# Turning position tiles in halves of 64 rows into a ring of five PSUM banks, and a reordered start, in a hybrid attention and Fourier encoder

## The chip, the cores and the metric

The kernel runs on one NeuronCore of one Trainium2 chip. The metric is the device time of one launch in microseconds (us). Engines are named as in the profile: PE (TensorE, matrix multiplication and transposes into PSUM), DVE (VectorE), ACT (ScalarE), POOL (GpSimd) and SP, which here only issues transfers. PSUM is the accumulator memory that PE writes; it has banks of 128 partitions by 512 float32 values.

## The reference

Two layers, each of which normalises its input, mixes it, multiplies it by a SiLU gate, maps it back and adds it to the residual. The rows are one prompt of 2048 positions and one sample of 512, both 1024 wide.

- Layer 0 is windowed attention, 16 query heads in 4 groups, with a position bias from a table (`rel_bias`) and a sink logit for each head.
- Layer 1 is Fourier mixing: for each of four groups of 256 channels, the real part of the two-dimensional discrete Fourier transform over positions and channels.
- A final normalisation follows: `x * rsqrt(mean(x*x) + 1e-6) * g`.

```python
def rmsnorm(x, g):
    xf = x.astype(jnp.float32)
    inv = lax.rsqrt(jnp.mean(xf * xf, axis=-1, keepdims=True) + RMS_EPS)
    return (xf * inv * g.astype(jnp.float32)).astype(x.dtype)
```

## The kernel before, in words

Lines are those of the kernel before, as in its profile. Almost every product of two float32 matrices is made of three products of a reduced float32 format: each operand is split into a high part (a copy on ACT) and a low part (a subtraction on DVE), and `matmul3` (L92, matmuls at L95) multiplies high by high, high by low and low by high. So an operand of PE is ready when ACT and then DVE are through with it.

**The order.** A scheduler writes each engine's instructions into one list when the kernel is built, and every engine runs its list in order. `after(a, b)` asks that `a` stands behind `b`, and `seq(name, ins)` chains instructions by a name; both give an order and not a wait between engines. What an instruction waits for follows from the tiles it reads and writes.

**The start** (L214 to L268). Twelve matmuls on an `idle` tile come first. The first key weight is requested in two halves, the first on SP ahead of everything else, the second on ACT; `g0s`, the norm's weight in a layout of 128 partitions by 8, is requested on ACT as single values; then the tiles `xk` of the transposed input come on SP. ACT and DVE make `h` (L220, L221) and the weight's parts (L253, L254), and PE multiplies them. `bias_rows` (L262) multiplies a one-hot matrix by the bias table in float32 (`bp`, L271). The rest of attention is not touched by the change, except that `bank` is shared.

**Position steps** (from about 1060 us the second layer, from about 1340 us these). The transform over positions is split into `k1` (0 to 8) and a second factor of 128. `position` (L1330) computes for one `k1` two tiles `u`, the rows `k1` and `16 - k1`; for 0 and 8 it is one tile each. It works in two halves of channels `hf`. In each half PE writes a cosine part `Ap` and a sine part `Bp` (six products each with two inputs, three with one), ACT copies from `Ap` (L1354, L1357), and DVE adds or subtracts `Bp` (L1358 to L1361). At the end DVE multiplies each `u` by its gate (L1364). The inputs `gp` are split by ACT and DVE at L1324, and their sums and differences (L1184, L1651 to L1655) are DVE's work too.

A `u` must be turned before PE can multiply it by the output weights. There are two forms:

- `step` (L1551) for p0 and p8, p4, and p2: it runs `position`, then `finish` for the first tile that is still pending from the step before, then `split_T` (L960, transposes L967) for the new tiles, then `finish` for the other pending tile. `finish` (L1384) is 48 matmuls `fo` of 512 columns, two additions to the residual on DVE (L1392), and `normed` (L1373): squares on ACT, a power on POOL, the scaling on DVE (L1376).
- `Outs` (L1397) for `k1` of 6, 1, 7, 3 and 5: `turn` (L1403, transposes L1409) turns the two tiles into four banks; `own` (L1416, L1417) makes the parts of one, `sums` (L1426, L1433) of their sums and differences; `products` (L1442) has the output products `Wo`, `Zo` and `Xo` with residual additions at L1457. Its hooks let the next `position` and the next tile's turns in between.

Each turned bank, `Ap` and `Bp` come from `bank` (L77), which takes the next of five tiles of one bank in the pool `psum3`. A full tile takes eight transposes of 128 by 128, so a block of two tiles takes 16.

Of the kernel before, what the change touches and what calls it, by code (L numbers as in the profile page):

```python
# [19 lines left out]
P = 128  # L20
# [8 lines left out]
WARM = 12  # L29
BIG = 1.0e30  # L30
# [12 lines left out]
def encoder(  # L43
# [19 lines left out]
    ACT.dma_start(g0s, g0.rearrange("(k p) -> p k", p=P))  # L63
# [13 lines left out]
    def bank(name):  # L77
        return banks[-1].tile([P, 512], F32, tag="bank", name=name)

# [12 lines left out]
    def matmul3(out, a, b, start, stop, more=False):  # L92

        for i, j in ((0, 0), (0, 1), (1, 0)):
            pe(PE.matmul(out, a[i], b[j], start=start and i + j == 0, stop=stop and i == 1, skip_group_check=more))  # L95
# [10 lines left out]
    def load_w(c, n, name, lo_engine=None, late=None, w32=None):  # L106
# [15 lines left out]
        if lo_engine is None:  # L122

            for i in range(4):
                cs = slice(i * 256, i * 256 + 256)
                POOL.tensor_tensor(w[:, 1, cs], w32[:, cs], f32(w[:, 0, cs]), ALU.subtract)
        else:
            lo_engine.tensor_tensor(w[:, 1], w32, f32(w[:, 0]), ALU.subtract)
# [4 lines left out]
    stage, res_tile, ready, chain, last_fetch = [], [], {}, {}, [None]  # L133
# [15 lines left out]
    def attention_phase():  # L149

        with ExitStack() as es:
# [6 lines left out]
            def stats(c):  # L158
# [7 lines left out]
                def one(i):  # L166

                    if i:
                        sq = ACT.activation(xs[i - 1], xs[i - 1], AF.Square, accum_out=ss[:, i - 1 : i])

                        if c > 1:
                            seq(ACT, sq)
                        else:
                            after(sq, last_exp[0])
                    while len(xs) < min(nt, i + (2 if c > 1 else 1)):
                        t = len(xs)
                        xs.append(xtile([P, D], F32, f"xs{c}_{t}"))
                        after(SP.dma_start(xs[t], x[tok + t * P : tok + (t + 1) * P, :]), last_exp[0])
# [5 lines left out]
            def spread(c, inv, place=None):  # L184
# [9 lines left out]
                for i0 in range(0, nt, step):  # L194
# [4 lines left out]
                    ACT.copy(invb[:, i0 * P : (i0 + m) * P], ps[:, : m * P])  # L199
                return invb  # L200

            def make_h(c, invb, between={}):
# [4 lines left out]
                for k in range(KD):  # L207
# [6 lines left out]
                    SP.dma_start(xk[:, :n], xT[k * P : (k + 1) * P, tok : tok + n])  # L214
# [8 lines left out]
                    after(lo, last_u[1])  # L223
                    hs.append((h[:, 0], h[:, 1]))
# [19 lines left out]
            last_u = [None, None]  # L244
# [4 lines left out]
            def half(i):  # L249
                cs = slice(i * 512, i * 512 + 512)  # L250
                (SP, ACT)[i].dma_start(wk32[:, cs], w_in[8, :, cs])
                return lambda: (
                    tc.keep_in_program_order(ACT.copy(wk[:, 0, cs], wk32[:, cs])),  # L253
                    DVE.tensor_tensor(wk[:, 1, cs], wk32[:, cs], f32(wk[:, 0, cs]), ALU.subtract),  # L254
                )

            halves = [half(i) for i in range(2)]
            halves[0]()
            early = [(wk[:, 0], wk[:, 1])]
            hs, halo = make_h(0, None, {0: halves[1], 3: lambda: early.append(load_w(0, 9, "k0_1", DVE))})  # L260

            def bias_rows():  # L262
# [4 lines left out]
                SP.dma_start(rb[:32], rel_bias)  # L267
                oh = ap.tile([33, 512], F32, tag="s", bufs=2, name="oh")  # L268
                SP.dma_start(oh, onehot)
                bp = bank("bp")  # L270
                PE.matmul(bp[:NH], rb, oh, start=True, stop=True)  # L271
# [5 lines left out]
                SP.dma_start(sk, bass.AP(sink.tensor, sink.offset, [[0, P], [1, NH]]))  # L277
# [24 lines left out]
            def kv_proj(c, hs, halo, norms=None, early=None):  # L302
# [40 lines left out]
                if norms is not None:  # L343
                    wv.append(load_w(c, 10, f"v{c}_0", DVE))
                    inv = norms()
# [7 lines left out]
                for i0 in range(0, len(blocks), 4):  # L353
# [10 lines left out]
                    for i, (src, c0, b) in enumerate(group):  # L364
# [3 lines left out]
                        if inv is not None:  # L368
                            sc = ap.tile([P, 1], F32, tag="vsc", bufs=2, name=f"vsc{c}_{b}")
                            DVE.tensor_scalar(sc, inv[:, i : i + 1], 0.5, None, ALU.mult)  # L370
# [63 lines left out]
            def attention(c, p, res, uTs):  # L434
# [17 lines left out]
                def sinks():  # L452
# [4 lines left out]
                    if p:  # L457
                        seq(ACT, ends)

# [330 lines left out]
            def first_norms():  # L790
                bias.extend(bias_rows())
                return [s() for s in stats(0)][-1]
# [140 lines left out]
    def fourier_phase(tail):  # L933
        with ExitStack() as es:
# [43 lines left out]

            def sumsq(src, name, place=lambda ins: None):
# [111 lines left out]
            def prod(out, a, b, ks, first):  # L1091

                for k in ks:
                    cs = slice(k * P, (k + 1) * P)
                    matmul3(out, (a[0][:, cs], a[1][:, cs]), b[k], first and k == 0, k == 3, not first)
# [129 lines left out]
            banks.append(es.enter_context(tc.tile_pool(name="psum3", bufs=5, space=PSUM, reuse_waits="tile")))  # L1225
# [76 lines left out]
            def gated(name, r, place):  # L1302
# [3 lines left out]
                if r[2] is None:  # L1306
                    SP.dma_start(s2, rows(src, (r[0] - off, r[1])))
# [20 lines left out]
            last_b = [None]  # L1328

            def position(name, tab, gr, gs, tiles, loads=None, parts=None, between=None, later=None):  # L1330
# [31 lines left out]
                for u, s2 in zip(us, s2s):  # L1362
                    if later is None:
                        DVE.tensor_tensor(u, u, s2, ALU.mult)  # L1364
# [8 lines left out]
            def normed(x2, r):  # L1373

                inv = sumsq(x2, f"f{r[0]}")
                after(DVE.scalar_tensor_tensor(x2, x2, inv[:, 0:1], gfb, ALU.mult, ALU.mult), last_b[0])  # L1376
                SP.dma_start(out_rows(r), x2)
# [6 lines left out]
            def finish(uT, r):  # L1384
                r0 = r[0]
                x2 = residual(r)
                for half in range(2):
                    ps = psum2.tile([P, 512], F32, tag="acc", name=f"fo{r0}_{half}")
                    for k in range(KD):
                        matmul3(ps, uT[k], wo[half * KD + k], k == 0, k == KD - 1)  # L1390
                    xs = x2[:, half * 512 : half * 512 + 512]
                    DVE.tensor_tensor(xs, xs, ps, ALU.add)  # L1392
                normed(x2, r)

            class Outs:  # L1397
# [6 lines left out]
                def turn(self, i, hf):  # L1404
                    u, r = self.us[i]
                    ps = bank(f"tr{self.n}_{i}{hf}")
                    for k in range(4):
                        c0 = (hf * 4 + k) * P
                        PE.transpose(ps[:, k * P : (k + 1) * P], u[:, c0 : c0 + P], ident)  # L1409
                    v = ps.rearrange("p (k q) -> p k q", k=4)  # L1410
                    self.ps[i, hf] = v[:, :, ::-1] if r[2] is not None else v

                def own(self, i, hf):
                    t = htile([P, 2, 512], F32R, f"tT{self.n}_{i}{hf}")
                    hi, lo = (t[:, j].rearrange("p (k q) -> p k q", k=4) for j in range(2))
# [4 lines left out]
                def sums(self, i):  # L1420
# [3 lines left out]
                    out = F[i] = self.pair[:, i in (2, 3)].rearrange("p (k q) -> p k q", k=4)  # L1424
# [8 lines left out]
                    DVE.tensor_tensor(out, a, b, op)  # L1433
# [3 lines left out]
                def operands(self):  # L1437
                    self.turn(0, 0)
                    self.own(0, 0)
                    self.turn(1, 0)  # L1440
                    self.turn(1, 1)
                    self.sums(1)  # L1442
                    self.sums(2)
                    self.turn(0, 1)
# [5 lines left out]
                def products(self, hooks, last=False):  # L1450
# [5 lines left out]
                    def add(t, half, ps):  # L1456
                        DVE.tensor_tensor(t[:, q[half]], t[:, q[half]], ps, ALU.add)  # L1457
# [16 lines left out]
                    add(xa, 0, X)  # L1474
                    hooks[2]()
                    if not last:
                        normed(xa, self.us[0][1])
                    else:

                        ya, yb = zt("ya"), zt("yb")  # L1480
                        turned = DVE.tensor_tensor(ya, xa, gfb, ALU.mult)
                        inv = sumsq(xa, "fa", lambda ins: after(ins, turned))
# [163 lines left out]
            G[0], G[8], G[4] = (r0, None), (r8, None), (g4r, g4s)  # L1646
            emit(0, 8)
# [47 lines left out]
            finish(*pend.pop(0))  # L1695
# [4 lines left out]
            def reads(k1):  # L1700

                gl = [zt(f"go{k1}_{i}") for i in range(2)]
                for hf in range(2):
                    cs = slice(hf * 512, hf * 512 + 512)
                    for g, src in zip(gl, god[k1]):
                        SP.dma_start(g[:, cs], src[:, cs])
# [129 lines left out]
```

## Time and profile before

| | us |
|---|---|
| median of 3 runs | 1582.07 (1581.98 to 1582.3) |
| profiled execution, its own time | 1581.38 |
| its span | 1579.4 |
| TensorE busy | 1569.0 |
| VectorE busy | 1153.0 |
| ScalarE busy | 876.5 |
| GpSimd busy | 446.1 |

The span is the time from the first to the last instruction in the trace of one execution. Busy is the time in which an engine has at least one instruction under way; matmuls overlap one another, so a matmul's duration (about 0.39 us for 512 columns) is longer than the time from its start to the next one's. In a row of the timeline, the first number is the start in us, the second the length of a run of like instructions, then come the engine, the line, the operation, the tile written and the tiles read, the shapes and the count; in square brackets is the time for which the engine stood idle before it, and what released it. The granted clock of TensorE was 0.999.

### The profile page before, as it was taken

The numbers are of one execution on the slowest core, as the hardware profiler recorded it, in microseconds if no ns is written. First come the engines' busy times: TensorE is split into PE (matmuls) and PEld (weight loads), VectorE is DVE, ScalarE is ACT, GpSimd is POOL, SyncE is SP. The second block draws the span as 40 slices with busy tenths as digits, with TensorE's granted clock in tenths as the row PEclk, the third lists the DMA queues.
The fourth block names the chain that finished last, engine by engine and source line by source line (L and its number), as shares of the span: only waits on it lengthen the run. The fifth ranks groups of instructions, "written<-read, shape, count | busy, mean of one in ns | idle before, by whom it ended". The sixth has DMA issues, their size and how long they took to land.

```text
span 1579.4 us, 27477 instructions
## 1 busy us (share of the span) xinstructions
PE 1569.0 (99%) x9755; PEld 1321.7 (84%) x9755; DVE 1153.0 (73%) x2790; ACT 876.5 (55%) x2093; POOL 446.1 (28%) x613
## 2 busy tenths in 40 slices
PE   9999999999999999999999999999999999999998
PEld 7888888888888888988888888888888888888886
DVE  6888655877548786378764587769878878989796
ACT  6688535776246784267852476646655554343242
POOL 2475642421404314024232242223112111010110
PEclk9999999999999999999999999999999999999999
DMA  7597696565856567656649556665557569557752
GB/s 292 199 335 287 228 361 211 207 248 204 297 209 221 207 236 264 232 203 225 248 165 334 216 209 223 248 252 203 204 207 255 178 220 405 187 182 299 282 206 80
DMA packets 101732, 373.89 MB, mean 237 GB/s; under 512 B 12267, under 2 KB 23019, under 8 KB 84188
## 3 DMA queue, kind: packets, MB, share of 16 engines
q1 hardware_dynamic: 82860, 298.04, 53.0%
q0 software_dynamic: 16400, 70.04, 11.5%
q10 hardware_dynamic: 2336, 4.07, 0.7%
q8 instruction: 77, 1.26, 0.3%
q14 instruction: 59, 0.48, 0.1%
HBM read 280.84 MB, written 91.26 MB: 236 GB/s over the span
## 4 chain that ended last, share of the span: by engine, by line
PE 96%; DVE 2%; ACT 1%; issue 0%; DMA 0%; POOL 0%; POOLq 0%; SPq 0%; DVEq 0%; ACTq 0%
PE gp L95 14%; PE qp L95 14%; PE spt L95 11%; PE op L95 7%; PE W L95 6%; PE av L557 6%; PE spt L472 6%; PE fo L95 5%; PE vp L95 3%; PE Wo L95 3%; PE Z L95 3%; PE pt L531 3%; PE z L95 2%; PE Zo L95 2%; PE X L95 2%; PE z L1079 1%
## 5 line engine op out<-in xcount | busy, mean ns | idle before, releaser
L95 PE MATMUL gp<-h,wg 128*128 128x512 f32 x960 | 237.6, 395 | 0.0
L95 PE MATMUL qp<-h,wq 128*128 128x512 f32 x960 | 237.0, 396 | 0.0
L491 DVE CUSTOM_DVE_ANT_0 S<-spt,b 128x385 f32<-128x385 f32 (+1 forms) x320 | 156.5, 528 | 104.3 <-PE spt L472 67.9
L95 PEld LDWEIGHTS gp<-h,wg 128*128 128x128 f32 x960 | 174.9, 188 | 37.2 <-issue 1.0
L95 PEld LDWEIGHTS qp<-h,wq 128*128 128x128 f32 x960 | 174.9, 188 | 36.5 <-issue 0.2
L499 ACT ACTIVATE S<-S 128x385 f32<-128x385 f32 (+1 forms) x320 | 188.8, 596 | 19.8 <-DVE S L491 19.5
L539 ACT CAST pts<-pt 128x384 fp32r<-128x384 f32 (+1 forms) x240 | 100.5, 458 | 168.2 <-PE pt L531 159.1
L540 DVE TENSOR_TENSOR pts<-pt,pts 128x384 fp32r<-128x384 f32 (+1 forms) x240 | 114.3, 520 | 23.4 <-ACT pts L539 22.2
L95 PE MATMUL spt<-wo,uT 128*128 128x512 f32 x480 | 120.5, 391 | 0.0
L581 POOL TENSOR_TENSOR uT<-o,uT 128x256 fp32r<-128x256 f32 x75 | 55.6, 741 | 229.0 <-ACT uT L580 228.9
L95 PE MATMUL op<-wo,uT 128*128 128x512 f32 x480 | 118.9, 391 | 0.0
L472 PE MATMUL spt<-kwin,qab 64*128 64x384 f32 (+1 forms) x960 | 118.4, 352 | 0.0
L557 PEld LDWEIGHTS av<-pts,v 128*128 128x128 f32 x576 | 101.4, 188 | 18.8
L557 PE MATMUL av<-pts,v 128*128 128x512 f32 (+1 forms) x576 | 115.7, 341 | 0.0
L95 PE MATMUL fo<-wo,tTu 128*128 128x512 f32 x480 | 115.6, 392 | 0.0
L95 PEld LDWEIGHTS op<-wo,uT 128*128 128x128 f32 x480 | 89.3, 188 | 18.6
L95 PEld LDWEIGHTS spt<-wo,uT 128*128 128x128 f32 x480 | 89.1, 188 | 18.4
L95 PEld LDWEIGHTS fo<-wo,tTu 128*128 128x128 f32 x480 | 88.2, 188 | 17.2 <-ACT wo L1591 0.4
L511 DVE TENSOR_SCALAR S<-S 128x384 f32<-128x384 f32 (+1 forms) x192 | 96.1, 501 | 6.8
L472 PEld LDWEIGHTS spt<-kwin,qab 64*128 64x128 f32 x960 | 74.6, 186 | 28.2 <-issue 25.7
L577 POOL TENSOR_TENSOR o<-o,s 128x256 f32<-128x256 f32 x75 | 55.4, 739 | 135.1 <-DVE o L575 134.7
L531 PEld LDWEIGHTS pt<-ident,S 64*128 64x128 f32 x1328 | 78.4, 138 | 4.3 <-issue 2.0
(330 smaller groups left out, 3196.8 us busy)
## 6 DMA issues: line engine op xcount, KB each, us to landing
wo<-wsd SPq DMA_DIRECT2D x32, 1024.0 KB, 4.9
wq<-wsd SPq DMA_DIRECT2D x31, 1024.0 KB, 7.4
wg<-wsd SPq DMA_DIRECT2D x31, 1024.0 KB, 5.0
x<-x1d SPq DMA_DIRECT2D x40, 512.0 KB, 3.4
b<-b21d SPq DMA_DIRECT2D x40, 512.0 KB, 6.3
b<-rowd SPq DMA_DIRECT2D x40, 384.0 KB, 4.3
xs<-in_x_dram SPq DMA_DIRECT2D x23, 512.0 KB, 6.6
s2d<-gt POOLq DMA_DIRECT2D x40, 256.0 KB, 4.7
```

What stands on the lines that cost most here:

```text
L95: pe(PE.matmul(out, a[i], b[j], start=start and i + j == 0, stop=stop and i == 1, skip_group_check=more))
L472: pe(PE.matmul(banks[j][:, 2 + k0 * P : 2 + k1 * P], res["q"][rows, qp, b * P : (b + 1) * P], kwin[g][rows, kp, b * P + k0 * P : b * P + k ...
L491: seq(DVE, DVE.tensor_tensor_reduce(out=s[:, e0:e1], in0=ps[:, 1 + e0 : 1 + e1], in1=st["bias"][:, j, 386 - e1 : 386 - e0][:, ::-1], scale ...
L499: last_exp[0] = seq(ACT, ACT.activation(s[:, e0:e1], s[:, e0:e1], AF.Exp, bias=s[:, 386:387], scale=-1.0, accum_out=s[:, 387:388]))
L511: seq(DVE, DVE.tensor_scalar(s[:, ks], s[:, ks], den, None, ALU.mult))
L531: pe(PE.transpose(ps[h][:, kb, j, :], ss[j][rows, 1 + kb * P : 1 + (kb + 1) * P], ident[rows, rows]))
L539: seq(ACT, ACT.copy(hi, ps[:, k0:k1]))
L540: seq(DVE, DVE.tensor_tensor(lo, ps[:, k0:k1], f32(hi), ALU.subtract))
L557: pe(PE.matmul(to, v, pt, start=n == part == 0, stop=part == 1 and n in (1, len(todo) - 1), skip_group_check=n > 1,))
L577: eng.tensor_tensor(o, o, s, ALU.mult)
L581: low = eng.tensor_tensor(lo, o, f32(hi), ALU.subtract)
L1079: PE.matmul(to, m[part][:, g * P : (g + 1) * P], ch[:, 0, :, odd * P : (odd + 1) * P], start=part == 0, stop=part == 1,)
```

## The change

1. **Turns in halves.** From the steps p0 and p8 on, the pool `psum3` is closed and one tile `ring` of five banks takes its place. `bank` gives its banks out in turn. `half_turns` turns a 128-row tile by transposes of 64 rows by 128 columns with a 64 by 64 identity: the upper half of the rows to one bank, the lower half to another, the two alternating. A block of two tiles has 32 of them in place of 16. All of them are chained by `seq("turns", ...)`.
2. **Where the turns stand.** In `step` the turns come behind the last matmul of the first pending `finish`, and the first product of the next `finish` behind the turns (`behind`). For p6 likewise. In `products` the T3 product is split: its first half, then the turns, then its second half.
3. **Order on DVE.** The addition of `Xo` stands behind both gate multiplies of the next `position`; the normalisation and its square stand behind `sums(4)`, one further addition behind `sums(2)`.
4. **The start.** The first `x` tile is requested first on SP. The first weight comes in two quarters and a half, the second in two halves; each part is requested behind an `x` tile. `g0` is loaded as 8 rows of 128 and turned by PE in the middle of the idle matmuls, of which there are 10 in place of 12, on a constant. The requests of the next tiles, statistics and the next weights are tied to these.
5. **Bias rows.** The table is split into two parts, and two products in the reduced format take the place of the float32 one; the one-hot matrix is copied on POOL, and its large constant becomes 2 to the power of 100.

```diff
     def bank(name):
+        if ring:
+            return ring[0][:, slot()]
         return banks[-1].tile([P, 512], F32, tag="bank", name=name)
+    def half_turns(tiles):
+        views = []
+        for src in tiles:
+            a, b = sorted((slot(), slot()))
+            two = ring[0][:, a : b + 1 : b - a]
+            views.append(two.rearrange("p h (k q) -> p k h q", k=KD))
+            for k in range(KD):
+                for h in range(2):
+                    hp = slice(64 * h, 64 * h + 64)
+                    seq("turns", PE.transpose(
+                        two[:, h, 64 * k : 64 * k + 64], src[hp, k * P : (k + 1) * P], ident[hp, hp]
+                    ))
+        return views
...
                 if pend:
-                    finish(*pend.pop(0))
-                new = [(split_T(u, f"u{r[0]}", r[2] is not None), r) for u, r in new]
+                    chain["turns"] = finish(*pend.pop(0))
+                new = turned(new)
...
                     for k in range(KD):
-                        matmul3(ps, uT[k], wo[half * KD + k], k == 0, k == KD - 1)
+                        end = matmul3(
+                            ps, uT[k], wo[half * KD + k], k == 0, k == KD - 1, behind=None if half or k else chain.get("turns")
+                        )
...
-                    add(xa, 0, X)
+                    whole = add(xa, 0, X)
+                    for ins in gated_by[-2:]:
+                        after(whole, ins)
+                    chain["turns"] = prod(W, S[3], ft["T3"], (0, 1), False)
                     hooks[2]()
                     if not last:
-                        normed(xa, self.us[0][1])
+                        normed(xa, self.us[0][1], chain["sums", 4])
...
-                    prod(W, S[3], ft["T3"], four, False)
-                    add(xb, 1, W)
+                    prod(W, S[3], ft["T3"], (2, 3), False, chain["turns"])
+                    ins = add(xb, 1, W)
+                    if not last:
+                        after(ins, chain["sums", 2])
...
+            p3.close()
+            psum4 = es.enter_context(tc.tile_pool(name="psum4", bufs=1, space=PSUM, reuse_waits="tile"))
+            ring.append(psum4.tile([P, 5, 512], F32, name="ring"))
             emit(0, 8)
...
-            finish(*pend.pop(0))
+            chain["turns"] = finish(*pend.pop(0))
             o.operands()
```

The start and the bias rows:

```diff
-            idle = ap.tile([P, 512], BF16, tag="s", bufs=2, name="idle")
-            DVE.memset(idle, 0.0)
+            idle = nc.const_aps.tensor(1.0, [P, 512], BF16)
             ps = bank("idle")
+            g0r = ap.tile([KD, P], F32, tag="tmp", bufs=2, name="g0r")
+            ACT.dma_start(g0r, g0.rearrange("(k p) -> k p", p=P))
+            gp = bank("g0t")[:, :KD]
             for i in range(WARM):
-                PE.matmul(ps, idle[:, :P], idle, start=True, stop=True)
+                warm = PE.matmul(ps, idle[:, :P], idle, start=True, stop=True)
+                if i == WARM // 2:
+                    turned = PE.transpose(gp, g0r, ident[:KD, :KD])
...
+            parts = [(0, 0, 256), (0, 256, 512), (0, 512, 1024), (1, 0, 512), (1, 512, 1024)]
+            def piece(i):
+                t, c0, c1 = parts[i]
...
+                load = (SP if i else ACT).dma_start(w32[:, cs], w_in[8 + t, :, cs])
+                if i:
+                    after(load, last_x[0])
+                hi = ACT.copy(w[:, 0, cs], w32[:, cs])
+                lo = DVE.tensor_tensor(w[:, 1, cs], w32[:, cs], f32(w[:, 0, cs]), ALU.subtract)
...
+            piece(0)
+            hs, halo = make_h(0, None, {k: (lambda i=i: piece(i)) for k, i in ((0, 1), (1, 2), (3, 3), (5, 4))})
...
-                PE.matmul(bp[:NH], rb, oh, start=True, stop=True)
+                for part in range(2):
+                    PE.matmul(bp[:NH], rbs[:, part], ohr, start=not part, stop=part == 1)
```

More of the change, by code (lines that the diff above doesn't have):

```diff
@@ L247, in attention_phase @@
             wk32 = stage[0]("w32k0_0")
[L249 to L259, printed above, removed]
@@ L458, in sinks @@
                         seq(ACT, ends)
+                    elif not c:
+                        after(ends, last_inv[0])
                 def span(b):
@@ L977, in split_T, with turned @@
                 return out
+            def turned(us):
+                out = [[] for u in us]
+                views = half_turns([u for u, r in us])
+                for hf in range(2):
+                    for (u, r), v, parts in zip(us, views, out):
+                        t = main.tile([P, 2, 512], F32R, align_bytes=LINE, tag="hT", bufs=8, name=f"tTu{r[0]}_{hf}")
+                        src = v[:, 4 * hf : 4 * hf + 4]
+                        if r[2] is not None:
+                            src = src[:, :, ::-1, ::-1]
+                        hi, lo = (quarters(t[:, i]) for i in range(2))
+                        ACT.copy(hi, src)
+                        DVE.tensor_tensor(lo, src, f32(hi), ALU.subtract)
+                        parts += [(t[:, 0, k * P : (k + 1) * P], t[:, 1, k * P : (k + 1) * P]) for k in range(4)]
+                return [(parts, r) for parts, (u, r) in zip(out, us)]
             def sumsq(src, name, place=lambda ins: None):
```

129 lines of the change are left out of this document (82 added, 47 removed).

## The prediction

> **What bounds the kernel now.** I read the page first: the share of each engine and the chain that ended last.
>
> ```profile
> span 1579.4 us, 27477 instructions
> PE 1569.0 (99%) x9755; PEld 1321.7 (84%) x9755; DVE 1153.0 (73%) x2790; ACT 876.5 (55%) x2093; POOL 446.1 (28%) x613
> PE 96%; DVE 2%; ACT 1%; issue 0%; DMA 0%; POOL 0%; POOLq 0%; SPq 0%; DVEq 0%; ACTq 0%
> ```
>
> TensorE never rests (99% busy, 96% of the chain). So there are two ways to move the time: fewer microseconds of TensorE work, or a place where TensorE now has to wait. An engine with spare time as a whole (DVE 73%) can still be late at one place. I therefore read the stages that the change touches one by one: busy times by stretch, then the timeline of PE and of DVE around each block of transposes.
>
> ```profile
> 1390.00:1450.00 60.00, 59.46 (x304) 49.97 (x303) 55.96 (x77) 21.48 (x41) 5.03 (x7) 1.00 0.54 199
> 1499.00:1523.10 24.10, 24.10 (x125) 20.43 (x125) 21.15 (x37) 10.08 (x21) 4.06 (x4) 1.00 0.57 191
> ```
>
> After the length the columns are PE, PEld, DVE, ACT and POOL busy, the granted clock, DMA share and GB/s. TensorE is full here, but DVE is at 93% and 88% (55.96 of 60, 21.15 of 24.1), and it makes the tiles that are turned. The question is how much matmul work stands between the last position matmul and the turns.
>
> **The half turns.** A block turns two tiles, 16 transposes of 128x128 now, 32 of 64x64 later.
>
> ```profile
> 1443.54 0.87 PE L95 MATMUL Bp<-gp,tbp 128*128 128x256 f32 x6
> 1444.25 4.95 PE L95 MATMUL fo<-wo,tTu 128*128 128x512 f32 x21
> 1449.05 1.91 PE L1409 MATMUL tr<-ident,up 128*128 128x128 f32 x16
> 1450.71 1.62 PE L95 MATMUL fo<-wo,tTu 128*128 128x512 f32 x6
> ```
>
> A block now takes 1450.71 − 1449.05 = 1.66 us, 0.104 per transpose, and a 512-column matmul 4.80 / 21 = 0.229. The attention layer has 64-row transposes that go in pairs into two banks:
>
> ```profile
> 698.94 0.61 PE L95 MATMUL qp<-h,wq 128*128 128x512 f32 x2
> 699.48 0.44 PE L472 MATMUL spt<-kwin,qab 64*128 64x384 f32 x2
> 701.04 0.21 PE L531 MATMUL pt<-ident,S 64*128 64x64 f32 x1
> 701.37 0.22 PE L531 MATMUL spt<-ident,S 64*128 64x64 f32 x1
> 701.52 1.65 PE L95 MATMUL qp<-h,wq 128*128 128x512 f32 x6
> ```
>
> The pt row opens six pairs and the spt row is the last of their twelve. The sixth pair's second half starts 0.33 after the first pt; some 0.02 of it is the offset within a pair, so five steps take 0.31, 0.062 a pair. From the sixth pair's first half to the next full-height matmul 0.17 passes. Entering costs 0.09: of the two L95 the second starts about 699.17, and the next matmul 0.31 later, where 0.229 is the step (0.61 less a step gives 0.38 for one matmul). A new block is then 15 × 0.062 + 0.17 + 0.09 = 1.19, and saves 0.47; eight blocks (p0/p8, p4, p2 and five pairs of outputs) save **3.8 us** (3.0 if 0.1 more goes at the edges, 4.5 if entry is free).
>
> The Trainium skill speaks against this part: "TensorEngine Tiling (Array Packing)", section Tiling Modes, says that changing the tiling mode, not just the tile, drains the engine. The attention rows agree that both edges cost something, but little (0.09 in, 0.17 to the next start). By a full drain, estimated as the whole length of the last instruction at each edge (a matmul's 0.38 us in place of 0.31, a transpose's 0.22 in place of 0.17), the eight blocks would save about 2.9 us instead.
>
> **Where the turns stand now.** The saving is small against what the new order does. In the built program the turns of a `step` follow the whole `finish` of the first pending tile and precede every matmul of the next; in `products` they follow the first half of T3. All transposes are chained, and the five banks count as one tile, so a turn also waits for every earlier read of that tile. Each place needs its own look at what covers DVE's last work.
>
> *Steps p0 and p8.*
>
> ```profile
> 1359.29 0.52 PE L95 MATMUL Bp<-gp,tbp 128*128 128x256 f32 x3
> 1359.64 4.04 PE L95 MATMUL fo<-wo,tTu 128*128 128x512 f32 x17
> 1363.53 1.91 PE L967 MATMUL tru<-ident,up 128*128 128x128 f32 x16
> 1359.91 0.42 DVE L1360 TENSOR_TENSOR up<-up,Bp 128x254 f32<-128x254 f32 x1
> 1360.25 0.68 DVE L1392 TENSOR_TENSOR x<-x,fo 128x512 f32<-128x512 f32 x1
> 1360.85 0.41 DVE L1361 TENSOR_TENSOR up<-up,Bp 128x254 f32<-128x254 f32 x1
> 1361.18 1.22 DVE L1184 TENSOR_TENSOR ev<-ev,z 128x1024 f32<-128x1024 f32 x1
> 1362.31 1.22 DVE L1364 TENSOR_TENSOR up<-up,s2p 128x1024 f32<-128x1024 f32 x1
> ```
>
> Now 17 matmuls (3.9 us) lie between the last Bp and the turns, and the gate multiply (L1364) ends at 1363.53, just in time. In the built program one matmul is left there. p0's turns wait for p8's last L1361, the ring's last reader: 0.33 + 0.60 + 0.41 after the Bp result less the 0.23 of that matmul, at least 1.3, and up to 2.5 since L1651 and L1654 (1.13 each, the step from 1361.18 to 1362.31) stand ahead of it on DVE; I take 2.2. p8's turns then wait for L1652 and the gate, 1.13 + 1.22, less p0's own half block of 0.55: 1.8. Together **4.0** (3.1 to 4.3).
>
> *p4* keeps 31 matmuls (7.1 us) of cover, more than the 5.2 that the longest such chain below takes, and stalls nothing. *p2* keeps 21 (4.8 us) where it has 34:
>
> ```profile
> 1409.67 7.88 PE L95 MATMUL fo<-wo,tTu 128*128 128x512 f32 x34
> 1413.10 1.22 DVE L1364 TENSOR_TENSOR up<-up,s2p 128x1024 f32<-128x1024 f32 x1
> ```
>
> Turns would be reached at 1414.48 and the gate is over at 1414.32, level; but three of the combinations of L1184 (1.13 each) now stand ahead of it in DVE's order, and the second half's Ap waits for the first half's reads. I take **1.4** (0 to 2.0).
>
> *p6.* Before, 21 matmuls (rows of 1444.25 above) follow the last Bp; in the built program none, because the 48 of the next `finish` must come behind the turns.
>
> ```profile
> 1435.15 1.28 DVE L1376 SCALAR_TENSOR_TENSOR x<-x,invf,gfb 128x1024 f32<-128x1024 f32 x1 [0.44 <-POOL invf L89]
> 1444.52 0.42 DVE L1358 TENSOR_TENSOR up<-up,Bp 128x254 f32<-128x254 f32 x1 [0.96 <-PE Bp L95]
> 1445.52 1.22 DVE L1364 TENSOR_TENSOR up<-up,s2p 128x1024 f32<-128x1024 f32 x1
> 1446.65 0.41 DVE L1361 TENSOR_TENSOR up<-up,Bp 128x254 f32<-128x254 f32 x1
> ```
>
> DVE starts 0.27 after PE is free of Bp, then three additions (1.0), gate (1.13), addition (0.33), normalisation of the tile just finished (1.20: its 1.28 less the 0.08 by which a step, 1445.52 to 1446.65, is shorter than a duration) and second gate (1.22): 5.2 us in which PE has nothing. If the normalisation slips behind, 4.0. Ahead of that, Ap of the second half waits for the residual add of the last fo and one more addition: 0.15 (0.38 less a step) + 0.60 + 0.41 = 1.2, with no other matmul placed there. Together **6.4** (4.0 to 7.0). The queue behind is all of PE; what was cover now runs later and hides nothing.
>
> *The outputs.* p1 keeps 30 matmuls ahead of its turns: no stall. For p7, p3 and p5 the period before shows
>
> ```profile
> 1493.49 0.88 PE L95 MATMUL Bp<-gp,tbp 128*128 128x256 f32 x6
> 1494.20 1.09 PE L95 MATMUL Zo<-wo,S 128*128 128x512 f32 x4
> 1499.00 1.91 PE L1409 MATMUL tr<-ident,up 128*128 128x128 f32 x16
> 1494.47 0.42 DVE L1358 TENSOR_TENSOR up<-up,Bp 128x254 f32<-128x254 f32 x1 [1.31 <-PE Bp L95]
> 1496.93 0.68 DVE L1457 TENSOR_TENSOR x<-x,Zo 128x512 f32<-128x512 f32 x1
> 1497.53 1.22 DVE L1364 TENSOR_TENSOR up<-up,s2p 128x1024 f32<-128x1024 f32 x1
> ```
>
> From the end of Bp's issue (1494.20) to the turns are 4.8 us, 21 matmuls; the second gate ends at 1498.75, 0.25 early. In the built program Bp of the second half comes so late that two of Xo and six of T3 follow, 8 × 0.229 = 1.8 us. DVE's chain, without the Zo add (0.60), ends 4.55 − 0.60 = 3.95 after 1494.20, so the turns stand **2.2** late, three times: 6.6 (1.6 to 2.7 each: the lower if the multiply's result is seen at its last write, the upper if the first half's Ap also waits). The add of Xo behind both gates costs nothing, since DVE would idle while PE turns.
>
> **The start.**
>
> ```profile
> 0.73 0.39 SPq L251 DMA_DIRECT2D w32k<-in_w_in_dram  x1
> 1.18 1.90 SPq L214 DMA_DIRECT2D xk<-in_xT_dram  x4
> 3.83 0.62 ACT L253 CAST wk<-w32k 128x512 fp32r<-128x512 f32 x1 [0.70 <-DMA w32k<-in_w_in_dram]
> 5.96 0.72 ACT L220 ACTIVATE h<-xk,g0s 128x512 fp32r<-128x512 f32 x1 [1.52 <-DMA xk<-in_xT_dram]
> 6.74 0.50 PE L95 MATMUL spt<-h,wk 128*128 128x512 f32 x1 [0.95 <-ACT h L220]
> L271 PE MATMUL bp<-oh,rb 33*16 33x512 f32 x2 | 1.0, 594 | 0.0
> ```
>
> What is asked for first is usable 3.1 us later (0.73 to 3.83); x, asked second, after 4.8. Put first, x is there about 4.1; with the same 0.78 from h to the first matmul that one starts near 4.9 to 5.3. PE then runs as now, minus short waits for the quarters: **−1.5** (−2.3 to −0.5). The bias product becomes two passes of 0.229: **−0.5** (0 to −0.6). The extra copy `ohr` is on POOL, 28% busy; stats and weight order change only who is first on queues that wait for nothing here.
>
> **Sum.** 4.0 + 1.4 + 6.4 + 6.6 = 18.4 of new waits, less 3.8, 1.5 and 0.5: **+12.6 us**. The profiled run is at 1581.38 (span plus 2.0); the median of 1582.07 is 0.7 above. 1582.07 + 12.6 = **1594.7**. With all low ends 11.9 − 4.5 − 2.3 − 0.6 = +4.5, 1586.6; with all high ends 21.4 − 3.0 − 0.5 = +17.9, 1600.
>
> **Rivals.**
> 1. *The outputs' waits don't form* (DVE reaches the second gate while T3 runs, as DVE has 3 us free in each 24.1): 12.6 − 6.6 = +6.0, 1588. Against it, the chain's rows are back to back behind Bp.
> 2. *Faster*: every turn finds its tile ready, and only the savings stay: −3.8 − 1.5 − 0.5 = −5.8, 1576.3. The mechanism is DVE's order alone: if it takes the second gate straight after L1361, and the position matmuls' results come early enough, no turn waits. It decides at the second gate of p6: either it is done when PE is through with Bp, or PE waits. For it speaks that DVE is idle 12% of the outputs' stretch; against it, that a list on PE is run in order and one matmul or none stands at p0/p8 and p6.
> 3. *The halves don't overlap* because they are halves of one tile: 32 × 0.104 = 3.3 instead of 1.19 per block, +17 more, 1612. The two halves go to two banks, as at L531, which speaks against it.
>
> **How the numbers follow.** Main case 0.62 (own range 1587 to 1600), rival 1 0.16, rival 2 0.12, rival 3 0.06, and 0.04 that waits and savings cancel. Differences up to 0.2% (3.2 us) can't be told from none. Faster 0.12, same 0.04, slower 0.84. The range leaves out rival 2 and most of rival 3: 1580 to 1601.
>
> **What will show it.** Right: idle time of PE ahead of the transposes, released by DVE's up, about 5 us at p6, 2 at p7, p3 and p5, 4 in p0/p8; a block of about 1.2 us; the first real matmul near 5.1. Wrong: PE busy through those places, or a block of 1.7 us or more.

## The result, and the profile after

| | before | after |
|---|---|---|
| median | 1582.07 us | 1609.17 us (1607.09 to 1609.75, 5 runs) |
| ratio, 95% interval | 1 | 1.0169 [1.0158, 1.0181] |
| span of the profiled execution | 1579.4 us | 1607.1 us |
| TensorE busy | 1569.0 us | 1576.6 us |

The kernel is 27.1 us slower, where 12.6 were forecast: the direction was right, the time lies beyond the range. The page of the changed kernel begins so:

```profile
span 1607.1 us, 27758 instructions
PE 1576.6 (98%) x9882; PEld 1323.4 (82%) x9882; DVE 1153.0 (72%) x2793; ACT 880.8 (55%) x2096; POOL 442.6 (28%) x614
```

The span is 27.7 us longer. TensorE's time without work grew from 10.4 us (1579.4 − 1569.0) to 30.5, by 20.1: that is the waits. But its busy time grew too, by 7.6 us, although each block of transposes should have become shorter. The first part was forecast and the second was not.

The timeline of PE at five of the places where blocks of transposes (the turns) stand shows the waits. In brackets stands the idle time ahead of a row and its releaser.

```profile
1364.81 0.40 PE L120 MATMUL fo<-wo,tTu 128*128 128x512 f32 x1
1367.41 0.71 PE L97 MATMUL ring<-ident,up 64*128 64x64 f32 x16 [2.20 <-DVE up L1442]
1369.60 1.12 PE L97 MATMUL ring<-ident,up 64*128 64x64 f32 x16 [1.47 <-DVE invf L113]
1370.64 5.73 PE L120 MATMUL fo<-wo,tTu 128*128 128x512 f32 x15
...
1426.46 1.20 PE L97 MATMUL ring<-ident,up 64*128 64x64 f32 x32 [1.12 <-DVE up L1445]
1427.60 0.73 PE L120 MATMUL fo<-wo,tTu 128*128 128x512 f32 x2
...
1453.38 1.68 PE L120 MATMUL ring<-gp,tbp 128*128 128x260 f32 x12 [1.20 <-DVE up L1442]
1460.60 1.97 PE L97 MATMUL ring<-ident,up 64*128 64x64 f32 x32 [5.53 <-DVE up L1445]
1462.49 1.78 PE L120 MATMUL fo<-wo,tTu 128*128 128x512 f32 x4
...
1518.33 1.94 PE L97 MATMUL ring<-ident,up 64*128 64x64 f32 x32 [2.62 <-DVE up L1445]
1520.20 2.40 PE L120 MATMUL Wo<-fT,S 128*128 128x512 f32 x6
```

p0 waits 2.20 and p8 1.47 (the releaser named there is the instruction behind p8's gate multiply, which ended at 1369.54), p2 1.12, p6 1.20 and 5.53, p7 2.62 (p3 and p5 the same). Now look at the second numbers. The 32 transposes of p2 take 1.20 us, those of p6 and p7 1.97 and 1.94; p0's 16 take 0.71, p8's 1.12. Six matmuls behind p7's block take 2.40 where the six ahead of its wait, from 1514.17, take 1.54. The same instructions run slower behind the longer waits. The busy time by stretch says why; the column ahead of the last two is the granted clock, as a mean over the stretch.

```profile
1340.00:1360.00 20.00, 19.66 (x95) 1.00 0.64 224
1360.00:1370.00 10.00, 6.33 (x53) 0.91 0.37 135
1370.00:1380.00 10.00, 10.00 (x46) 0.75 0.57 181
1380.00:1390.00 10.00, 9.58 (x49) 1.00 0.20 77
...
1450.00:1460.00 10.00, 3.87 (x22) 0.85 0.99 362
1460.00:1470.00 10.00, 9.40 (x62) 0.81 1.00 404
1510.00:1520.00 10.00, 7.38 (x63) 0.92 0.45 119
1520.00:1530.00 10.00, 10.00 (x45) 0.91 0.54 208
```

Before, the clock was 1.00 in all of these stretches. From 1370 to 1380 TensorE is busy all the time and does 46 instructions where it did 54.

DVE ahead of p6's turns, in the changed kernel:

```profile
1455.58 0.42 DVE L1439 TENSOR_TENSOR up<-up,ring 128x254 f32<-128x254 f32 x1 [1.24 <-ACT up L1438]
1455.91 0.41 DVE L1440 TENSOR_TENSOR up<-up,ring 128x254 f32<-128x254 f32 x1
1456.24 0.41 DVE L1441 TENSOR_TENSOR up<-up,ring 128x254 f32<-128x254 f32 x1
1456.57 1.22 DVE L1445 TENSOR_TENSOR up<-up,s2p 128x1024 f32<-128x1024 f32 x1
1457.71 0.41 DVE L1442 TENSOR_TENSOR up<-up,ring 128x254 f32<-128x254 f32 x1
1458.04 1.28 DVE L1457 SCALAR_TENSOR_TENSOR x<-x,invf,gfb 128x1024 f32<-128x1024 f32 x1
1459.23 1.22 DVE L1445 TENSOR_TENSOR up<-up,s2p 128x1024 f32<-128x1024 f32 x1
```

This is the chain that the prediction set up for p6, in its order: three additions, a gate, an addition, the normalisation, the second gate, back to back and with nothing on PE.

The start, on PE:

```profile
0.77 2.72 PE L272 MATMUL idle<-const-bfloat16-1.0 128*128 128x512 bf16 x6 [0.77 <-PEq L1911]
3.42 0.27 PE L274 MATMUL g0t<-ident,g0r 8*128 8x8 f32 x1
3.62 1.89 PE L272 MATMUL idle<-const-bfloat16-1.0 128*128 128x512 bf16 x4
5.92 13.14 PE L120 MATMUL spt<-h,wk 128*128 128x512 f32 x48 [0.41 <-ACT h L247]
18.98 0.63 PE L325 MATMUL bp<-ohr,rbs 33*16 33x512 f32 x2
19.54 0.62 PE L120 MATMUL spt<-wv,h 128*128 128x256 f32 x3
```

In the kernel before:

```profile
18.23 1.03 PE L271 MATMUL bp<-oh,rb 33*16 33x512 f32 x2
19.19 0.62 PE L95 MATMUL spt<-wv,h 128*128 128x256 f32 x3
```

The first real matmul starts at 5.92 instead of 6.74, yet the first product of the values (`spt<-wv,h`) at 19.54 instead of 19.19.

### The profile page after: what moved, and what is told of

Read it like the earlier page. It is cut to its first block, busy times and chain, and to the rows that moved or that the text cites. A ratio compares the mean times of both kernels' runs of the same rounds, so it can differ in the third digit from the quotient of the medians.

```text
span 1607.1 us, 27758 instructions
## 1 busy us (share of the span) xinstructions
PE 1576.6 (98%) x9882; PEld 1323.4 (82%) x9882; DVE 1153.0 (72%) x2793; ACT 880.8 (55%) x2096; POOL 442.6 (28%) x614
## 3 DMA queue, kind: packets, MB, share of 16 engines
q8 instruction: 78, 1.28, 0.3%
```

## The experiments

Theory A: the waits are those of the prediction, and the rest is TensorE at half clock behind them. Theory B: the rest is work that the change added. All times are medians; intervals are those of the ratio to the kernel before on the same chip.

**Fill the waits.** Matmuls with a zero operand keep PE busy where it waits for DVE. They add zeros to sums that are open.

```diff
+zero(W, {1: 10, 7: 10, 3: 10}.get(self.n, 0))   # ahead of the turns of p7, p3, p5
...
+zero(ps, 9, True)                                # p0, and 5 more ahead of p8
...
+zero(ps6, 28, True)                              # p6
```

> The changed kernel with 66 more matmuls of 128x512 whose moving operand is zero, added into sums that are open anyway, in the places where TensorE waits for the turns: 9 and 5 in p0/p8, 28 around p6, 10 each ahead of p7, p3 and p5 (0.216 each, less than each wait). Theory (the waits cost twice: the wait itself, and a half clock afterwards): the waits stay, blocks take 1.13 in place of 1.90, matmuls after them 0.227 in place of 0.427; that gives back 1.5 in each of the three outputs, 1.4 in p6 and 2.7 in p0/p8, 8.6 us in all, 1600.5. Rival (the long blocks come from the half transposes or from readers of the ring, not from the idle time): no change or slower, 1609 to 1611.

1600.97 us, 1.0115 [1.0098, 1.0132]: 8.2 us faster by doing more. The transposes behind the filled wait of p7, in its timeline of PE:

```profile
1511.82 2.12 PE L1476 MATMUL Wo<-const-float32-0.0,const-bfloat16-1.0 128*128 128x512 bf16 x9
1514.37 1.21 PE L101 MATMUL ring<-ident,up 64*128 64x64 f32 x32 [0.43 <-DVE up L1449]
1515.51 1.65 PE L124 MATMUL Wo<-fT,S 128*128 128x512 f32 x6
```

The wait for DVE is still there, from 1511.82 to 1514.37. But 32 transposes take 1.21 instead of 1.94 and six matmuls 1.65 instead of 2.40. Theory A holds.

**How much idle time is needed.** Fewer zeros, first 2, 4 and 6 in the three outputs, then 3 in each.

```diff
-zero(W, {1: 10, 7: 10, 3: 10}.get(self.n, 0))
+zero(W, {1: 2, 7: 4, 3: 6}.get(self.n, 0))   # first kernel
+zero(W, {1: 3, 7: 3, 3: 3}.get(self.n, 0))   # second kernel
```

> As the run that fills the waits, but with only 2, 4 and 6 zero matmuls ahead of the turns of p7, p3 and p5, which leaves idle times of about 2.2, 1.8 and 1.3 us. Theory (a wait has to be long before the clock halves; 1.47 and 2.2 in a row did it in p0/p8, 1.1 in p2 did not): p5 keeps blocks of 1.13, p7 falls to 1.9; p3 lies between what the traces show so far, either may come. Rival (any wait over 1 us halves the clock where DVE is this busy): all three at 1.9.

> As the run that fills the waits, with 3 zero matmuls in each of the three outputs, which leaves an idle time of 1.96 us three times. Theory (a fixed length between 1.74 and 2.18 us halves the clock): all three blocks alike, all 1.13 or all over 1.5. Rival (it depends on where the idle time falls): some of each.

1601.32 and 1604.1 us ([1.0123, 1.016] for the second). An idle time of 2.18 us was followed by a slow block, 1.74 and 1.30 were not. With 1.95 three times over, the clock fell behind the block in one output, near its end in the next and in its middle in the last. Three equal waits, three different points: the clock does not count from the wait's start. Call a return to full clock a rise and its opposite a fall. The steps from matmul to matmul in the traces give the rule. At full clock a step is 0.227, at half clock 0.427; one step *s* in between holds the rise, which lies (*s* − 0.227) / 0.468 behind that step's start. In the changed kernel:

| place | step that holds the rise: start and length | rise at | distance to the rise above, in units of 3.4133 us |
|---|---|---|---|
| start | 9.43, 0.371 long | 9.74 | |
| p0 and p8 | 1374.65, 0.423 | 1375.07 | 400.0 |
| p6 | 1463.51, 0.369 | 1463.81 | 26.0 |
| p7 | 1521.65, 0.326 | 1521.86 | 17.0 |
| p3 | 1548.81, 0.391 | 1549.16 | 8.0 |
| p5 | 1576.27, 0.315 | 1576.46 | 8.0 |

The six rises lie on one grid of 3.413 us that runs through the whole execution. The trace also holds the granted clock itself as a record, and that agrees: its rises are the same to 0.03 us, and its stretches at half clock last 3.413 or 6.827 us (from 1368.30 to 1375.00 the clock reads 0.50, from 1375.10 to 1378.00 1.00). The falls lie on it too: p7's transposes go from 0.062 to 0.107 a pair at 1518.45, one period ahead of 1521.86. In the run with 1.95 the rises are at 1517.45, 1544.82 and 1572.13, and the pairs get slower at 1541.41 and 1568.72, again one period earlier. So the clock is set for each period by how busy the one before it was: with 1.95 us idle in a period it halved, with 1.74 it did not. Other traces narrow this. With 1.91 (p6 of the changed kernel, from 1455.07 to a period's end at 1456.98) the clock halved; with 1.80 (ahead of `Zo` at 1459.96, in the run with halves alone below) it did not. A longer wait of 2.06 that lay across the end of a period, 0.84 in one and 1.23 in the next (ahead of `Zo` at 1460.79, in the run with p6 free below), left it at full. To rise took more than not to fall: the period from 1368.24 to 1371.65 of the changed kernel had 1.36 us idle ahead of p8's turns, and the clock stayed low for another one.

"TensorE: Matmul & The Clock Gate" in the Trainium skill, Part 1, "What's actually happening", describes a free-running window of 3413 ns, and the traces show just that. It lets the clock fall after a whole idle window; here 1.95 of 3.41 us were enough, so the measurement decides.

**The start by itself.** First the transpose of `g0` behind all idle matmuls, then the new start and bias rows (parts 4 and 5 of the change) in the kernel before.

```diff
             for i in range(WARM):
                 warm = PE.matmul(ps, idle[:, :P], idle, start=True, stop=True)
-                if i == WARM // 2:
-                    turned = PE.transpose(gp, g0r, ident[:KD, :KD])
+            turned = PE.transpose(gp, g0r, ident[:KD, :KD])
+            after(turned, warm)
```

> The changed kernel with the small transpose of g0 behind all ten idle matmuls in place of in their middle. Theory (the gap that this transpose makes among the idle matmuls keeps the clock at half until 9.5 us): the clock rises near 4.6 to 5.0, the eight matmuls that took 0.427 take 0.227, first real matmul some 0.6 later: 0.6 to 1.4 us faster over the first 20 us. Rival (ten idle matmuls on a constant don't raise the clock, whatever stands between): the matmuls up to 9.5 us stay at 0.427, and the start is 0.3 to 0.6 us slower.

> The kernel before with the new start and the bias rows in two reduced products, nothing else. Theory (the half clock at the start takes back what the earlier first matmul gains): +0.2 to +0.6 us against before, 1582.2 to 1582.8. Rival (the start does gain, and the shift of 0.35 seen in the changed kernel has another origin): 1580 to 1581.

The first took 1608.33 us, 1.0164 [1.0147, 1.0181]: 0.8 below the changed kernel, and that is within the spread. The clock was up near 5 us and the first product of the values came at 18.23, 1.3 earlier. The second took 1581.03 us, 0.9993 [0.9984, 1.0003]: no measurable change, so the loss that was expected did not come. Its profile has that product at 17.64, 1.55 ahead of before, with the same broken row of idle matmuls and the clock up by 3.5. So the break alone is not what kept the clock down in the changed kernel. In that execution a period of the grid ended at 9.74 − 3.41 = 6.33, and it held the wait of 0.41 us ahead of 5.92; the clock stayed low for another period. In the run with the new start and halves in the steps (below) a period ended nearly there, at 6.20, with no wait in it, and the clock rose. But idle time alone is not the measure: the period that raised the clock in the start alone, up to 3.48, had 0.70 us idle ahead of its first matmul. So this reading of the start is argued; no run set the grid's position. And of the 1.55 us only 0.25 are left at 1438: TensorE waits at later places instead, such as 0.31 ahead of the products `X<-b,tTb` at 1089 and 0.26 ahead of an `fo` at 1334.

**The two causes of the waits.** The prediction saw that the turns had lost their cover (the matmuls that PE still has to do while DVE makes the tile), and put it to the new order. Three kernels separate the order (part 2) from the ring as one tile (part 1): the changed kernel without the order requests; the changed kernel with five separate bank tiles in place of `ring`; and the latter without the request at p6. Separate banks also mean that ACT and DVE read each turned pair in two pieces, which gives both more to do.

```diff
-matmul3(ps, uT[k], wo[half * KD + k], k == 0, k == KD - 1, behind=None if half or k else chain.get("turns"))
+matmul3(ps, uT[k], wo[half * KD + k], k == 0, k == KD - 1)      # first kernel; likewise in products
...
-two = ring[0][:, a : b + 1 : b - a]
+two = [bank("trh0"), bank("trh1")]                               # second and third kernel
...
-chain["turns"] = finish(*pend.pop(0))
+finish(*pend.pop(0))                                             # third kernel, p6 only
```

> The changed kernel without the order that was asked for around the turns: they need not follow the whole first finish nor precede the next, and T3 is one product again; half turns, ring and start stay. Theory (the place of the turns makes the waits): p0/p8, p2 and p6 lose their waits of 3.7, 1.1 and 5.5 and the half clock behind them; in the outputs six more matmuls (1.4 us) stand ahead of the turns but none between the turns and the next product, so that a wait of 1.0 to 1.3 moves behind them: 1590 to 1594. Rival (the ring's waits as one tile are what delays): p0/p8 and p6 keep waits of over 2 us, 1600 or more.

> The changed kernel with all its order requests, but the half turns go to five separate banks in place of one ring tile. In the built program the second half's Bp then stands 17 matmuls ahead of the turns in p7, p3 and p5 (8 with the ring), and 17 stand there in p0/p8 (1 with the ring); p6 still has none. Theory (the waits at p0/p8, p2 and the outputs come from the ring being one tile, which makes Ap of the second half wait for all reads of the first; only p6's comes from the place of the turns): waits only at p6, 4.0 to 5.5 and the half clock behind, blocks 1.13: 1583 to 1586. Rival (the place of the turns is the cause everywhere): waits of over 1.5 in p0/p8 and the outputs stay, 1595 or more.

> As the run with separate banks, and p6's turns need not stand behind the whole finish nor ahead of the next; 21 matmuls then stand ahead of them. Theory: no wait over 0.6 us in the position steps; savings of 4.2 for the blocks and about 1 for the start stay: 1576 to 1578, faster than before. Rival (something else in the change costs time): 1581 or more.

| | median, us | interval | waits ahead of the turns of p0/p8, p2, p6, and of p7, p3 and p5 (outputs), us |
|---|---|---|---|
| changed kernel | 1609.17 | 1.0158 to 1.0181 | 3.67, 1.12, 5.53, 2.62 each |
| without the order | 1594.57 | 1.006 to 1.0098 | 0, 0, 0, 1.26 each |
| separate banks | 1587.38 | 1.0023 to 1.0054 | 0, 0, 4.25, 0.28 to 0.48 each |
| separate banks, p6 free | 1583.84 | 1.0007 to 1.0026 | 0, 0, 0, to 0.48 each |

At p0/p8 and p2 it takes both: either one alone leaves no wait. In the outputs the ring does it, and without the order a further 1.00 and 0.65 us follow each block. There p1, which waits nowhere in the changed kernel, has such waits too: 1.48, 0.95 and 0.65. At p6 the order alone makes 4.25; the ring adds 1.28 to that, and the 1.20 ahead of `Ap` needs both. The 0.45 ahead of p2's `Ap`, for its input `gp`, is 0.41 with separate banks, so neither the ring nor lost cover explains it. With separate banks 16 matmuls lie between the last `Bp` and p3's turns (10 and 6 below, from the third kernel), with the ring 8:

```profile
1520.80 0.40 PE L128 MATMUL Bp<-gp,tbp 128*128 128x256 f32 x2
1521.04 2.48 PE L128 MATMUL Xo<-wo,tT 128*128 128x512 f32 x10
1523.35 1.52 PE L128 MATMUL Wo<-fT,S 128*128 128x512 f32 x6
1525.36 1.20 PE L96 MATMUL trh<-ident,up 64*128 64x64 f32 x32 [0.48 <-DVE up L1450]
```

Five banks that count as one tile let `Ap` and `Bp` be written only when every earlier read of any bank is through, so the position matmuls come later in the list and the cover comes before them.

The last kernel was forecast at 1576 to 1578 and missed that. Its blocks take 1.13 to 1.15 us, but PE stands idle for 2.06 us ahead of p6's `Zo` and for 1.22 ahead of the turns in the outputs, and the matmuls of the output products take some 2 us more in all than before, idle time aside. The wait at `Zo` comes back below; the rest stays open.

**Halves alone.** The half turns into separate banks in the kernel before, with its order and with the reads in two pieces; then only in the three steps; then the latter with the new start.

```diff
+two = [bank("trh0"), bank("trh1")]
+for k in range(KD):
+    for h in range(2):
+        hp = slice(64 * h, 64 * h + 64)
+        PE.transpose(two[h][:, 64 * k : 64 * k + 64], u[hp, k * P : (k + 1) * P], ident[hp, hp])
```

> The kernel before, its start and its order requests unchanged, with turns in halves of 64 rows into banks of their own (five separate tiles in place of one ring); each turned bank pair is then read in two pieces by ACT and DVE. Theory (a half block takes 1.13 in place of 1.66, and the ring is what harms): 8 blocks give 4.2, less waits of up to 1 us behind the turns where the scheduler leaves under 3 matmuls there (three outputs): 1578 to 1581. Rival (half turns themselves cost time, in reads or in edges): 1583 or more.

> The kernel before with half turns into separate banks only in p0/p8, p4 and p2, where over 25 matmuls follow the turns; the outputs turn as before. Theory (the half turns gain 0.43 a block where cover is left, and it was the outputs' readers that gave it back): 1.3 us faster than before, 1580.1 to 1581. Rival (readers in two pieces cost as much here): no change.

> As the run before it, with the new start too. Theory (the start gives 0.5 to 1.5 by the execution, as the clock rises early or late): 1579 to 1580.5, faster than before by over 0.1%. Rival: the start gives nothing in the median, 1580.5 to 1581.

1584.71 [1.001, 1.0028], 1582.12 [0.9992, 1.001] and 1582.16 us [0.9993, 1.0011]. All three lie above what the theory gave. Every block of 32 took 1.14 us instead of 1.66, and the first two kernels were 1.5 and 1.0 us ahead at 1446 (0.4 of the 1.5 stood ahead of the first block). The lead was then lost at one place, where the first kernel waits for 1.80 us. That kernel lost some 2 us more in the outputs, with 0.88, 0.35 and 0.35 us idle behind turns; whether the reads in two pieces cost this, as its rival had it, no run separates. The place is seen in the second of these kernels, PE and DVE:

```profile
1456.20 2.88 PE L95 MATMUL Wo<-wo,tT 128*128 128x512 f32 x12
1460.24 2.09 PE L95 MATMUL Zo<-fT,S 128*128 128x512 f32 x8 [1.15 <-issue]
```

```profile
1456.20 0.68 DVE L1445 TENSOR_TENSOR tT<-tr,tT 128x512 fp32r<-128x512 f32 x1
1459.45 1.29 DVE L1420 TENSOR_TENSOR x<-x,fo 128x512 f32<-128x512 f32 x2 [2.57 <-PE Wo L95]
```

`Zo` waits for its bank, which DVE still has to read, and DVE stands idle for 2.57 us ahead of that read; before it stood at 1457.75. The releaser named is a matmul that had long been done, so it was another, and the add also needs the residual `x` from DRAM. SP's own queue in this kernel:

```profile
1436.22 3.08 SPq L1568 DMA_DIRECT2D fT<-fT1d  x4
1439.39 7.61 SPq L1568 DMA_DIRECT2D fT<-fT2d  x4
1449.92 0.34 SPq L1405 DMA_DIRECT2D out_dram<-x  x1
1450.31 1.41 SPq L1409 DMA_DIRECT2D x<-x1d  x3
```

and in the kernel before:

```profile
1439.11 0.32 SPq L1381 DMA_DIRECT2D x<-x1d  x1
1439.53 2.68 SPq L1540 DMA_DIRECT2D fT<-fT1d  x4
1442.30 6.60 SPq L1540 DMA_DIRECT2D fT<-fT2d  x4
```

The residual `x` used to be requested at 1439.11, ahead of eight loads of `fT` (512 KB each, as `x` itself). In the list built with the shorter blocks it stands behind them, at 1450.31.

**That request put back.**

```diff
-SP.dma_start(f32(t), f32(ftd[w][k]))
+after(SP.dma_start(f32(t), f32(ftd[w][k])), last_res[0])
...
+xs6 = [residual(r) for u, r in pend]
-finish(*pend.pop(0))
+finish(*pend.pop(0), xs6[0])
```

> The run before with the halves in the position steps and the new start, and both residual loads of the second finish (x for p6's two halves) requested on SP ahead of the eight fT loads instead of behind them. The theory that the late x took back what the steps had gained: the 1.44 us wait before p6's Zo is gone, DVE's add of that half stands where it stood in the kernel before, and the time is 1579.3 to 1580.8 us, ahead of the kernel before by the 1.3 us of the steps and whatever the start leaves. The rival, that Zo's bank waits for something else (the end of DVE's own work in the steps): Zo still begins at about 1460.2 and the time stays at 1581.5 to 1582.5.

The wait is gone:

```profile
1456.31 2.88 PE L94 MATMUL Wo<-wo,tT 128*128 128x512 f32 x12
1459.03 2.88 PE L94 MATMUL Zo<-fT,S 128*128 128x512 f32 x12
```

Its DVE add stands at 1458.10. The time was 1580.67 us (11 runs) beside 1581.58 for the kernel before (15 runs), 0.9996 [0.9987, 1.0005]. The median lies where the theory put it, but the interval contains 1: it is not shown to beat the kernel before. In the trace 0.85 of the lead at `Zo` became 0.42 by the next matmul rows at 1464.

## Why the prediction was right, and where it was wrong

| term of the sum | forecast, us | measured, us |
|---|---|---|
| wait at p0 and p8 | 4.0 | 2.20 + 1.47 = 3.67 |
| wait at p2 | 1.4 | 1.12, and 0.45 ahead of `Ap` = 1.57 |
| wait at p6 | 6.4 | 1.20 + 5.53 = 6.73 |
| waits in the outputs | 6.6 | 3 × 2.62 = 7.86 |
| p4, and `Ap` of p0 and p8 | 0 | 0.42 + 0.34 = 0.76 |
| eight blocks | −3.8 | about −3.3 at full clock |
| start and bias rows | −2.0 | +0.35 in the profiled execution |
| clock behind the waits | no term | about 8.6 |
| sum | 12.6 | 26.2 of 27.7 in the spans; 1.5 not assigned |

- **The waits were right**, 19.8 against 18.4 (19.4 without p2's 0.45, which is no lost cover) and each close to its own forecast. Following DVE's list behind the last `Bp` gave them: which of its instructions stand ahead of the turns, at their steps, less the matmuls left on PE.
- **The blocks**: 1.19 was forecast for a block with the step into it; 1.13 to 1.14 is measured from the first transpose to the next matmul at full clock. At p4, where nothing waits, the matmul ahead of the block steps 0.319 where 0.23 is usual, so the 0.09 for entering was right; the one behind it steps 0.338, before 0.314. Without these edges a block saves 0.53, with them 0.42; eight at 0.42 are 3.3. That lies between the 3.8 of the sum and the 2.9 of its estimate by a full drain. Rival 3's halves that don't overlap are refuted by 32 transposes in 1.20.
- **The step that failed is the sum itself: "18.4 of new waits, less 3.8, 1.5 and 0.5".** It priced the work behind each wait at its duration at full clock. A wait that leaves PE idle for 1.9 us or more of one period of 3.41 halves the clock for the next, which costs up to 1.6 more: p0 and p8 about 2.6 (two periods, less the idle time in them), each of p6 and the outputs about 1.5; 8.6 by the lengthened steps. Filling the waits gave 8.2 back. With this term the sum is 21.2, 1603.3 us; the range ended at 1601 because it had no bound for it.
- **The start was mis-sized.** First real matmul 5.1 forecast, 5.92 measured here (5.25 in the start alone). "PE then runs as now" failed: the first seven of its matmuls stepped at half clock, 0.427 us or more each, and at the values PE was 0.35 us behind instead of 2.0 ahead. The bias rows gave 0.4: from 18.98 to 19.54 are 0.56, before 0.96. Even where the start gained 1.55 us, nearly all of it was given back to waits later on.
- **The cause of the lost cover was named by half.** The prediction took the places of the matmuls from the built list and put them to the new order; the ring's reads came in at p0's turns and as delays of `Ap` at p2 and p6. The runs show that the ring as one tile, by moving the position matmuls in that list, is needed for every wait but 4.25 us of p6's.
- **Rival 1** fell, as the outputs' waits formed. **Rival 2** fell at the point it named: at p6 PE was through with `Bp` at 1455.07 and the second gate began at 1459.23.

## What to carry to other kernels

Where an order or a tile takes away the work that covers a vector chain, add up the wait, and then ask whether it fills over half of one clock period (here 1.91 of 3.41 us did, 1.80 did not): if so, the work behind it costs up to another 1.6 us. A pool of separate bank tiles and one tile with the same banks look alike in PSUM, but the second ties each write to the reads of all banks, and a list written ahead of time moves with it. A shorter block is worth nothing until the next thing is early as well; here that was one residual load, behind eight others on the same queue.

## What was unexpected in the hardware

- The clock of TensorE is set on a grid of 3.413 us that held through 1567 us of one execution to the last hundredth (400 periods between the rises at 9.74 and 1375.07). In these traces the threshold for halving lies between 1.80 and 1.91 us of idle time in one period.
- With the same new start the rise came between 3.5 and 6.2 us in eight traces, and at 9.5 and 9.7 in two, so the first products of the values differ by 1.9 us (17.64 to 19.54).
- The granted clock in the stretch from 0 to 10 us of the changed kernel reads 1.00, while its matmuls stepped at 0.427 or more until 9.43. The trace's record of the clock begins with the first rise, at 9.73, so there the column doesn't show what the steps show:

```profile
0.00:10.00 10.00, 8.82 (x20) 1.00 0.78 250
```
